# The sixteen tiles of the split activations, laid at sixteen distances of 16 bytes from multiples of 256

## Chip, cores and metric

The kernel runs on one core of one Trainium2 chip. The metric is the device time of one execution in microseconds, the median of several runs. A profile is one such execution, recorded instruction by instruction. On this chip TensorE (PE) multiplies matrices, VectorE (DVE), ScalarE (ACT) and GpSimd (POOL) do element-wise work, and SyncE (SP) starts transfers. SBUF is the on-chip memory: 128 partitions, in each of which an address counts bytes. A tile of 128 rows and 512 fp32 columns takes 2048 bytes of each partition.

## What is computed

A model of two layers on 512 tokens of width 1024. Each layer has a feed-forward block, a mixing block of three token mixers, and a second feed-forward block; a final norm ends it.

```python
for l in range(DEPTH):
    h = rms_norm(x, ffn1_norm[l])
    x = x + 0.5 * swiglu_ffn(h, ffn1_w_gate[l], ffn1_w_up[l], ffn1_w_down[l])
    h = rms_norm(x, mix_norm[l])
    (a_q, a_f, a_i, a_g, b_q, b_k, b_v, b_z, b_beta, b_a,
     c_q, c_k, c_v, c_g) = jnp.split(h @ w_in[l], SPLIT_IDX, axis=-1)
    o_a = hgrn2_mixer(...)
    o_b = gated_deltanet_mixer(...)
    o_c = retention_mixer(...)
    x = x + jnp.concatenate([o_a, o_b, o_c], axis=-1) @ w_out[l]
    h = rms_norm(x, ffn2_norm[l])
    x = x + 0.5 * swiglu_ffn(h, ffn2_w_gate[l], ffn2_w_up[l], ffn2_w_down[l])
return rms_norm(x, final_norm)
```

where `swiglu_ffn(h, wg, wu, wd) = (silu(h @ wg) * (h @ wu)) @ wd`, and the inner width is 2816. All data are fp32.

## The kernel before

The activations lie transposed: eight tiles `x` of 128 features by 512 tokens. For each dense product both factors are split in two parts that TensorE takes in its faster fp32r form: a rounded high part and the remainder as a low part. A product is then three matmuls, high by high, high by low and low by high (`mm3`, line 209), each pair with a weight load of its own. `split_x` (line 386) makes the sixteen tiles of the split activations, `xh0` to `xh7` on ACT and `xl0` to `xl7` on DVE; it is called by `prepare` after each block, once for each of the eight feature tiles. `split` (line 197) does the same for the weights, into tiles `hi` and `lo`.

Three groups of products read the split activations:

- `pg` and `pu`, the gate and up products of the four feed-forward blocks (`ffn`, line 445; matmul at line 215). `hi` or `lo` is stationary, a tile `xh` or `xl` streams through with its 512 columns.
- `ps_fm`, part of the input product of the mixing block (`dense_stream`, matmul at line 258), in the same form.
- `ps_tm`, the other part. Here 128 columns of `xh` or `xl` are stationary, and 256 columns of `hi` or `lo` stream. The first of these, called `t0` in the plan, has 264 columns (8 and 256 side by side).

Other dense products don't read them: `pd`, the down product, streams `ah` and `al`; `ps_out`, the output product, streams `mh` and `ml`. In the mixing block the mixers' own small matmuls, all of them fp32 (line 263), are woven between the matmuls of `ps_fm` and `ps_tm`.

The order on each engine is written by the program's scheduler when it is built. The pools take their memory one behind the other: constants, a pad, the split activations (`xsp`), raw weights, `hi`, `lo`, and the working tiles `m`. With the pad of 224 bytes, `xh0` starts at byte 23296 of a partition, 91 times 256. All sizes behind it are multiples of 256: 2048 for each of the sixteen tiles, 8192 for raw weights, 4352 for a tile `hi` or `lo` (`UNIT` of 1088 columns), 2048 for a working tile. So each of these tiles starts at a multiple of 256. What a matmul reads of them starts there too, since slices are taken at multiples of 512 or 1024 bytes, with one exception. In `t0` the tile `hi` holds four slices of 264 columns, which is 1056 bytes; slice j starts at 1056 j, which is 32 j bytes past a multiple of 256.

```python
t = pool.tile([P, UNIT], F32R, tag=tag, name=tag)
return t[:, 0:shape[1] * shape[2]].rearrange("p (k f) -> p k f", k=shape[1])
...
for j in range(4):
    xh, xl = self.xs[i * 4 + j]
    for m, (a, b) in enumerate(((xh, wh), (xl, wh), (xh, wl))):
        self.mmr(pss[t], a[:, tt], b[:, j, :],
```

Of the kernel before, what the change touches and what calls it, by code (L numbers as in the profile page):

```python
# [11 lines left out]
F32R = mybir.dt.float32r  # L12
# [7 lines left out]
P = 128  # L20
D = 1024
KD = D // P
T = 512
# [73 lines left out]

UNIT = 1088
PAD = 56
STEP = 1600  # L100
SLICE = 2200
LAT = 1.4
# [61 lines left out]
class Kern:  # L164
# [9 lines left out]
    def pool(self, name, bufs, **k):  # L174
        return self.tc.tile_pool(name=name, bufs=bufs, reuse_waits="tile", **k)
# [209 lines left out]

    def split_x(self, d, x, w):
        nc = self.nc
        h = self.xsp.tile([P, T], F32R, tag=f"xh{d}", name=f"xh{d}")
        l = self.xsp.tile([P, T], F32R, tag=f"xl{d}", name=f"xl{d}")
        nc.scalar.activation(h, x, AF.Copy, scale=w[:, d:d + 1])  # L390
        nc.vector.scalar_tensor_tensor(l, x, w[:, d:d + 1], h.bitcast(F32), ALU.mult, ALU.subtract)
        self.xs[d] = (h, l)
# [913 lines left out]
    def interleave(self, dense, waiting):  # L1306
# [3 lines left out]
        while more or any(waiting.values()) or running:  # L1310
# [5 lines left out]
            if r and (r[0] <= self.pe or not more):  # L1316
                self.pe = max(self.pe, r[0])
                self.done = self.pe
                with self.tc.high_priority(offset=PRIO[r[1]]):
                    if next(r[2], self) is self:  # L1320
                        running.remove(r)
                r[0] = max(self.done * LAT + self.pe * (1 - LAT), self.pe) + STEP
                continue
# [97 lines left out]
    def run(self):  # L1421
        nc, tc, io = self.nc, self.tc, self.io
        with ExitStack() as ctx:
# [4 lines left out]
            self.pad = pool("pad", 1)  # L1428
            self.pad.tile([P, PAD], F32, name="pad")
            self.xsp = pool("xsp", 1)  # L1430
# [92 lines left out]
```

## Time and profile before

| | |
|---|---|
| median of 3 runs (lowest, highest) | 2195.98 us (2189.47, 2198.14) |
| the profiled execution, its own time | 2199.5 us |
| its span, first to last instruction | 2197.7 us |
| mean granted TensorE clock | 0.989 |
| PE busy | 2164.1 us (98%), 13079 matmuls |
| DVE, ACT, POOL busy | 1147.4, 842.8, 498.6 us |

The page of the profile gives busy times of the engines, the chain of work that ended last, and groups of instructions. The chain is followed back from the last instruction, at each step to what released it; merged by line, it gives pieces with a start, a length and a count of instructions. The length of a piece over its count is the time from one matmul's start to the next one's. The durations of single matmuls in the groups overlap each other (a matmul of 512 columns has 389 ns there), so pace is read from starts, in the chain or the timeline, and not from durations. The timeline lists single instructions with their start and length in microseconds; PEld is the weight load that goes with a matmul. TensorE's granted clock, as a share of full speed, is 1.00 in nearly all of the span, and 0.50 in short stretches.

### The profile page before, as it was taken

The numbers are of one execution on the slowest core, as the hardware profiler recorded it, in microseconds if no ns is written. First come the engines' busy times: TensorE is split into PE (matmuls) and PEld (weight loads), VectorE is DVE, ScalarE is ACT, GpSimd is POOL, SyncE is SP. The second block draws the span as 40 slices with busy tenths as digits, with TensorE's granted clock in tenths as the row PEclk, the third lists the DMA queues.
The fourth block names the chain that finished last, engine by engine and source line by source line (L and its number), as shares of the span: only waits on it lengthen the run. The fifth ranks groups of instructions, "written<-read, shape, count | busy, mean of one in ns | idle before, by whom it ended". The sixth has DMA issues, their size and how long they took to land.

```text
span 2197.7 us, 31776 instructions
## 1 busy us (share of the span) xinstructions
PE 2164.1 (98%) x13079; PEld 1836.0 (84%) x13079; DVE 1147.4 (52%) x1980; ACT 842.8 (38%) x1319; POOL 498.6 (23%) x466
## 2 busy tenths in 40 slices
PE   8999999998999999999999999999999999999998
PEld 7888888887988788888888888888889888888888
DVE  5544335468497843433543343364866886434335
ACT  4323224555455422222432222254655544223225
POOL 2201012454323210101211010133633412101011
PEclk9999999999999999999999999999999999999999
DMA  5323234221223233232232322242211232323223
GB/s 155 124 79 115 77 106 145 68 78 40 59 59 107 92 100 96 77 115 77 96 115 96 96 96 96 82 150 63 73 45 53 70 106 84 108 94 99 96 86 125
DMA packets 197757, 203.08 MB, mean 92 GB/s; under 512 B 7626, under 2 KB 189292, under 8 KB 197612
## 3 DMA queue, kind: packets, MB, share of 16 engines
q1 hardware_dynamic: 197612, 201.05, 29.0%
q8 instruction: 103, 1.69, 0.3%
q14 instruction: 42, 0.34, 0.1%
HBM read 194.74 MB, written 6.29 MB: 91 GB/s over the span
## 4 chain that ended last, share of the span: by engine, by line
PE 89%; DVE 8%; ACT 1%; issue 1%; POOL 0%; DMA 0%; SPq 0%; DVEq 0%; ACTq 0%; POOLq 0%
PE pd L215 22%; PE pu L215 22%; PE pg L215 21%; PE ps_fm L258 8%; PE ps_tm L258 6%; PE ps_out L258 2%; PE ps_scan L263 1%; DVE aw L147 1%; DVE lo L147 1%; DVE x L147 1%; PE ps_ss L263 1%; PE ps_ao L263 1%; DVE xl L147 1%; PE ps_al L263 0%; PE ps_y L263 0%
## 5 line engine op out<-in xcount | busy, mean ns | idle before, releaser
L147 ACT CAST hi<-raw 128x1024 fp32r<-128x1024 f32 (+2 forms) x369 | 379.1, 1028 | 1104.3 <-PE pg L215 323.1
L147 DVE TENSOR_TENSOR lo<-raw,hi 128x1024 fp32r<-128x1024 f32 (+2 forms) x325 | 391.5, 1205 | 79.4 <-ACT hi L147 66.3
L147 POOL TENSOR_TENSOR g<-g,rstd 128x512 f32<-128x512 f32 x88 | 150.2, 1707 | 1131.9 <-ACT g L144 1131.9
L215 PE MATMUL pd<-ah,hi 128*128 128x512 f32 (+1 forms) x752 | 282.2, 376 | 0.0
L215 PE MATMUL pd<-ah,lo 128*128 128x512 f32 (+1 forms) x752 | 281.8, 375 | 0.0
L215 PE MATMUL pd<-al,hi 128*128 128x512 f32 (+1 forms) x752 | 281.8, 375 | 0.0
L215 PE MATMUL pg<-xl,hi 128*128 128x512 f32 x704 | 275.1, 391 | 1.0 <-DVE xl L147 1.0
L215 PE MATMUL pg<-xh,hi 128*128 128x512 f32 x704 | 274.5, 390 | 0.2 <-ACT xh L147 0.2
L215 PE MATMUL pu<-xh,lo 128*128 128x512 f32 x704 | 274.2, 390 | 0.3 <-DVE lo L147 0.3
L215 PE MATMUL pu<-xh,hi 128*128 128x512 f32 x704 | 274.4, 390 | 0.0
L215 PE MATMUL pg<-xh,lo 128*128 128x512 f32 x704 | 274.2, 390 | 0.0
L215 PE MATMUL pu<-xl,hi 128*128 128x512 f32 x704 | 274.0, 389 | 0.0
L147 DVE TENSOR_TENSOR u<-pu,g 128x512 f32<-128x512 f32 x88 | 60.9, 692 | 280.7 <-PE pu L215 265.2
L147 DVE SCALAR_TENSOR_TENSOR x<-pd,x 128x512 f32<-128x512 f32 (+1 forms) x104 | 67.4, 649 | 230.8 <-PE pd L215 230.5
L147 DVE TENSOR_TENSOR g<-pg,rstd 128x512 f32<-128x512 f32 x88 | 60.8, 691 | 206.8 <-PE pg L215 206.7
L215 PEld LDWEIGHTS pd<-ah,hi 128*128 128x128 f32 x752 | 141.5, 188 | 25.7
L215 PEld LDWEIGHTS pd<-ah,lo 128*128 128x128 f32 x752 | 141.6, 188 | 25.6
L215 PEld LDWEIGHTS pd<-al,hi 128*128 128x128 f32 x752 | 141.5, 188 | 25.5
L215 PEld LDWEIGHTS pg<-xl,hi 128*128 128x128 f32 x704 | 132.2, 188 | 29.4 <-DVE xl L147 2.3
L215 PEld LDWEIGHTS pg<-xh,hi 128*128 128x128 f32 x704 | 132.3, 188 | 27.9 <-ACT xh L147 0.4
L215 PEld LDWEIGHTS pu<-xh,lo 128*128 128x128 f32 x704 | 132.1, 188 | 28.0 <-DVE lo L147 0.8
L215 PEld LDWEIGHTS pu<-xh,hi 128*128 128x128 f32 x704 | 132.1, 188 | 27.7 <-ACT hi L147 0.2
(331 smaller groups left out, 3792.2 us busy)
## 6 DMA issues: line engine op xcount, KB each, us to landing
raw<-in_ffn_w_gate_dram SPq DMA_DIRECT2D x43, 1024.0 KB, 5.2
raw<-in_ffn_w_up_dram SPq DMA_DIRECT2D x43, 1024.0 KB, 5.1
raw<-in_ffn_w_down_dram SPq DMA_DIRECT2D x32, 1024.0 KB, 4.8
raw<-in_w_in_dram SPq DMA_DIRECT2D x20, 1024.0 KB, 5.1
raw<-in_w_in_dram SPq DMA_DIRECT2D x32, 512.0 KB, 3.7
raw<-in_ffn_w_down_dram SPq DMA_DIRECT2D x20, 768.0 KB, 4.4
xd<-x SPq DMA_DIRECT2D x16, 256.0 KB, 2.5
raw<-in_w_out_dram SPq DMA_DIRECT2D x16, 256.0 KB, 2.6
```

What stands on the lines that cost most here:

```text
L147: return f(*args, **kw)
L215: self.nc.tensor.matmul(ps, a[:, k, :], b, start=n == 0, stop=n == 3 * nk - 1)
L258: self.nc.tensor.matmul(ps, a, b, start=start, stop=stop)
L263: self.nc.tensor.matmul(ps, a, b, start=start, stop=stop)
```

## The change

The two tiles of one feature tile become one tile of twice 516 columns: `xh` is its columns 0 to 511, `xl` its columns 516 to 1027, and four columns behind each stay unused. So each of the sixteen tiles starts 2064 bytes behind the one before, which is 8 times 256 and 16 bytes. `xh0` stays at byte 23296; `xh` of feature tile d starts 32 d bytes past a multiple of 256, `xl` 32 d + 16. The sixteen together take 16 times 16, that is 256 bytes more, and every tile behind them moves up by 256 bytes and stays at a multiple of 256. The instructions of each engine and what they wait for stand in the same order as before.

```diff
 UNIT = 1088
 PAD = 56
+
+XSLOT = T + 4
 STEP = 1600
...
     def split_x(self, d, x, w):
         nc = self.nc
-        h = self.xsp.tile([P, T], F32R, tag=f"xh{d}", name=f"xh{d}")
-        l = self.xsp.tile([P, T], F32R, tag=f"xl{d}", name=f"xl{d}")
+        x2 = self.xsp.tile([P, 2 * XSLOT], F32R, tag=f"xs{d}", name=f"xs{d}")
+        h, l = x2[:, 0:T], x2[:, XSLOT:XSLOT + T]
         nc.scalar.activation(h, x, AF.Copy, scale=w[:, d:d + 1])
         nc.vector.scalar_tensor_tensor(l, x, w[:, d:d + 1], h.bitcast(F32), ALU.mult, ALU.subtract)
         self.xs[d] = (h, l)
```

## The prediction

> **What bounds the kernel now.** First the page: span, busy times, and the chain of work that ended last with its shares by engine and by line.
>
> ```profile
> span 2197.7 us, 31776 instructions
> PE 2164.1 (98%) x13079; PEld 1836.0 (84%) x13079; DVE 1147.4 (52%) x1980; ACT 842.8 (38%) x1319; POOL 498.6 (23%) x466
> PE 89%; DVE 8%; ACT 1%; issue 1%; POOL 0%; DMA 0%; SPq 0%; DVEq 0%; ACTq 0%; POOLq 0%
> PE pd L215 22%; PE pu L215 22%; PE pg L215 21%; PE ps_fm L258 8%; PE ps_tm L258 6%; PE ps_out L258 2%; PE ps_scan L263 1%; DVE aw L147 1%; DVE lo L147 1%; DVE x L147 1%; PE ps_ss L263 1%; PE ps_ao L263 1%; DVE xl L147 1%; PE ps_al L263 0%; PE ps_y L263 0%
> ```
>
> TensorE is the path: 89% of the chain. The lines that read the split x are `pu`, `pg`, `ps_fm` and `ps_tm`, together 57% of the span. Next the chain in order of time, which gives the pace of matmuls that wait for nothing (start, length, count).
>
> ```profile
> 65.75 5.44 PE pu L215 x24
> 71.19 5.44 PE pg L215 x24
> 234.89 43.52 PE pd L215 x192
> 2177.53 10.79 PE pd L215 x90
> ```
>
> A matmul of 512 columns follows the one before after 5.44 / 24 = 226.7 ns, the same in `pg`, `pu` and `pd` (43.52 / 192). The last row has 256 columns (the kernel's end): 10.79 / 90 = 119.9 ns. The difference is 106.8 ns for 256 columns, 0.417 ns a column; so 512 columns stream in 213.4 ns, and **13.3 ns a matmul are not streaming**. What are they? The timeline of a stretch at half clock, and the windows row with its clock (the 0.50):
>
> ```profile
> 441.30:443.00 1.70, 1.70 (x6) 1.31 (x5) 1.22 (x7) 0.00 (x0) 0.00 (x0) 0.50 0.41 146
> 441.29 0.63 PE L258 MATMUL ps_fm<-xh,hi 128*128 128x512 f32 x1
> ...
> 443.00 0.63 PE L258 MATMUL ps_fm<-xl,hi 128*128 128x512 f32 x1
> ```
>
> Four matmuls in 1.71 us are 427.5 ns each, and 512 columns at half speed are 426.8 ns. So the 13.3 ns are there at full clock only, where the stream of columns runs fastest. That speaks against a fixed pause and for two readers that get in each other's way: during each matmul the next weights are loaded.
>
> **The change part by part.** No instruction, wait or transfer is added, removed or moved, and all other tiles keep their distance from multiples of 256. What changes is where the 16 tiles start: all at multiples of 256 before, at 0, 16, ... 240 bytes past one now. So there is one term: what the start is worth to one matmul, times the matmuls that read these tiles and stand on the path.
>
> *The value.* One stage of before has its streaming tiles apart already: `t0`, where slice j of `hi` and `lo` starts 32 j bytes past a multiple of 256, and the stationary `xh`, `xl` at multiples of 256. Its timeline (start, length), at the first matmul of each slice, three matmuls each:
>
> ```profile
> 382.87 0.29 PE L258 MATMUL ps_tm<-hi,xh 128*128 128x264 f32 x1
> ...
> 383.24 0.28 PE L258 MATMUL ps_tm<-hi,xh 128*128 128x264 f32 x1
> ...
> 383.60 0.29 PE L258 MATMUL ps_tm<-hi,xh 128*128 128x264 f32 x1
> ...
> 383.97 0.28 PE L258 MATMUL ps_tm<-hi,xh 128*128 128x264 f32 x1
> ...
> 384.32 0.29 PE L258 MATMUL ps_tm<-hi,xh 128*128 128x264 f32 x1
> ...
> 384.69 0.28 PE L258 MATMUL ps_tm<-hi,xh 128*128 128x264 f32 x1
> ...
> 385.05 0.29 PE L258 MATMUL ps_tm<-hi,xh 128*128 128x264 f32 x1
> ...
> 385.42 0.28 PE L258 MATMUL ps_tm<-hi,xh 128*128 128x264 f32 x1
> ...
> 385.78 0.29 PE L258 MATMUL ps_tm<-hi,xh 128*128 128x264 f32 x1
> ...
> 386.15 0.28 PE L258 MATMUL ps_tm<-hi,xh 128*128 128x264 f32 x1
> ...
> 386.51 0.29 PE L258 MATMUL ps_tm<-hi,xh 128*128 128x264 f32 x1
> ...
> 386.87 0.28 PE L258 MATMUL ps_tm<-hi,xh 128*128 128x264 f32 x1
> ...
> 387.23 0.29 PE L258 MATMUL ps_tm<-hi,xh 128*128 128x264 f32 x1
> ```
>
> 36 matmuls take 387.23 - 382.87 = 4.36 us, 121.1 ns each. 264 columns stream in 110.0 ns; 11.1 ns are left. By slice, added over the three rounds and divided by nine: j = 0 (no distance) 1.11 us, 123.3 ns, so 13.3 left, exactly the rest found elsewhere; j = 1 (32 bytes) 1.08 us, 120.0, so 10.0; j = 2 (64) 1.10 us, 122.2, so 12.2; j = 3 (96) 1.07 us, 118.9, so 8.9. Starts are given to 10 ns, so each of these is good to about 1 ns. The aligned slice costs most. I take the mean over the four, a gain of 13.3 - 11.1 = **2.2 ns** a matmul, for all sixteen distances. Distances of 128 and more, and odd multiples of 16, which all `xl` get, no row shows. The bounds: above, all 13.3 ns go; below, as much is lost again, 13.3 ns, where a start costs instead. The value lies where the nearest rows, the four slices, lie.
>
> *How many.* The groups that keep shapes apart, the first and last of `pg` and `pu` (six rows of 704), then those of `ps_fm` and `ps_tm`:
>
> ```profile
> L215 PE MATMUL pg<-xl,hi 128*128 128x512 f32 x704 | 275.1, 391 | 1.0 <-DVE xl L147 1.0
> ...
> L215 PE MATMUL pu<-xl,hi 128*128 128x512 f32 x704 | 274.0, 389 | 0.0
> ...
> L258 PE MATMUL ps_fm<-xh,hi 128*128 128x512 f32 x320 | 133.2, 416 | 1.6 <-issue 1.6
> ...
> L258 PE MATMUL ps_tm<-lo,xh 128*128 128x256 f32 x448 | 130.3, 291 | 0.0
> ```
>
> `pg` and `pu`: 6 x 704 = 4224, nearly all on the path (their 43% of the span are 945 us, and 4224 x 226.7 ns are 958 us). 4224 x 2.2 ns = **9.3 us**. In the mixing block not all count, since in its middle DVE is the path. `ps_fm` has 8% of the span on the chain, 176 us or 776 matmuls at 226.7 ns; `ps_tm` 6%, 132 us or 1099 at 120 ns. Together 1875 of 2496, x 2.2 ns = **4.1 us**. In `ps_tm` it is the stationary side that is moved, and in `t0` both; I take the same value there.
>
> *What is late next.* Nothing, for a gain of 1%: the windows row of four pairs of `pg` and `pu` (length, then busy PE, PEld, DVE, ACT, POOL).
>
> ```profile
> 60.31:103.83 43.52, 43.52 (x193) 35.76 (x192) 18.77 (x23) 13.33 (x18) 9.24 (x6) 1.00 0.39 123
> ```
>
> DVE has 18.77 us of work in 43.52, ACT 13.33, and DMA engines are 39% busy.
>
> *The writers.* ACT and DVE write the 16 tiles, 40 times each in all, now at distances of 16 bytes. For other distances the trace has the convolution's taps, which read `braw` 4 and 8 bytes past a start:
>
> ```profile
> L147 DVE SCALAR_TENSOR_TENSOR bq<-braw,sv_b,bq 128x512 f32<-128x512 f32 x16 | 11.9, 744 | 2.8 <-POOL bq L147 2.7
> L147 DVE SCALAR_TENSOR_TENSOR xl<-ps_x,sv_n,xh 128x512 fp32r<-128x512 f32 x8 | 5.9, 742 | 0.0
> ```
>
> 744 against 742 ns: nothing. Those are reads; if a write paid even 100 ns, 40 of them would be 4 us, and few stand on the path. I take 0.
>
> *The sum.* 9.3 + 4.1 = 13.4 us. The profiled execution has 2199.5 us of its own (span 2197.7 and 1.8 around it) and would have 2186.1. It lies 3.5 us above the median; from the median, 2195.98 - 13.4 = **2182.6 us**, 0.6% faster.
>
> **The rivals.**
>
> *It doesn't matter where the tiles start.* Then the time stays at 2196. For it: `pd`, `pg` and `pu` have one pace to a few tenths of a nanosecond, while the weights they load lie in four buffers 17 x 256 bytes apart. But all of these are multiples of 256, and only `t0` tests anything else. Its slices could differ for their odd length of 264 columns, not for their start; against that stands that slice 0 has just the rest of the others. The Trainium skill speaks for this rival: "SBUF — State Buffer", section "SBUF: two separate sides", says that TensorE never waits for another reader, and names a lock on a port as the one contention among the engines; of the address it says nothing. By that rule the sum would be 0; the slices of `t0` speak against it as far as 264 columns can.
>
> *Odd starts cost.* If the stream is fetched in pieces of 32 bytes or more, a tile that starts in the middle of one has a broken piece at either end. All eight `xl` start so. A third of the 6099 matmuls on the path read `xl`, 2033. At another 13.3 ns each they lose 27.0 us, while the other 4066 gain 2.2 ns, 8.9 us: 18 us slower, 2214. It decides from 4.4 ns per `xl` matmul. Against it: slices 1 and 3 of `t0` start in the middle of 64 bytes and are the fastest two; for it: nothing in the trace starts at 16.
>
> *It gains much more.* If the sixteen distances on the whole do as well as slice 3, the gain is 4.4 ns x 6099 = 27 us, 2169; if all of the rest goes, 81 us, 2115. For it: the rest vanishes at half clock, so it can vanish. Against it: no slice lost more than a third of it. The Trainium skill, "TensorE: Matmul & The Clock Gate", section "Back-to-back issue gap", gives 512 columns at full clock about 215.8 ns. The trace has 226.7; at the page's figure the gain would be an estimated 66 us, 2130.
>
> **How the numbers follow.** Forecast (1 to 4 ns gained) 0.47; no effect 0.25; odd starts cost 0.15; much more 0.13. The forecast's own range is 2172 to 2190. A measurement of this kernel can tell about 0.5%, 11 us, from no change, so 2185 to 2207 is the same. Two thirds of the forecast lie below 2185, 0.31, and with the large gain faster has 0.44; the rest of the forecast, no effect and a small part of the odd starts make 0.43; slower has 0.13. The range of 8 in 10 runs from 2165, which leaves out most of the large gains, to 2206, which leaves out most of the odd starts.
>
> **What would show it.** In the profile after, the pieces of 24 matmuls of `pg` and `pu` should be 5.39 us instead of 5.44 (224.5 ns each), and `pd` should stay at 43.52 for 192. Within a piece the pace should change from tile to tile with the distance. If the pieces stay at 5.44, the start doesn't matter; if matmuls on `xl` alone are slower than 226.7 ns, odd starts cost. If the pace of `pg` falls and the time does not, my share of matmuls on the path is wrong. A changed `pd` would mean that more than the distances changed. The forecast is wrong above all if `t0` is no measure for 512 columns.

## The result, and the profile after

| | before | after |
|---|---|---|
| median of 4 runs (lowest, highest) | 2196.91 us (2189.47, 2198.14) | 2215.53 us (2212.42, 2219.84) |
| ratio after / before, 95% interval | | 1.0093 [1.0064, 1.0122] |
| profiled execution, its span | 2199.5, 2197.7 us | 2216.9, 2215.1 us |
| mean granted clock in it | 0.989 | 0.993 |

The change made the kernel 0.9% slower, where 0.6% faster was forecast. First the page after: span, busy times, chain by engine and by line.

```profile
span 2215.1 us, 31776 instructions
PE 2178.8 (98%) x13079; PEld 1829.5 (83%) x13079; DVE 1146.7 (52%) x1980; ACT 841.8 (38%) x1319; POOL 499.6 (23%) x466
PE 86%; DVE 9%; ACT 2%; issue 1%; DMA 1%; POOL 0%; SPq 0%; DVEq 0%; ACTq 0%; POOLq 0%
PE pu L217 22%; PE pg L217 22%; PE pd L217 21%; PE ps_fm L260 8%; PE ps_tm L260 5%; PE ps_out L260 2%; DVE aw L149 1%; PE ps_scan L265 1%; DVE lo L149 1%; PE ps_ss L265 1%; DVE x L149 1%; PE ps_ao L265 1%; DVE flo L149 1%; DVE ak L149 1%; ACT hi L149 0%
```

DVE, ACT and POOL have the busy times of before to within a microsecond, and TensorE is busy 14.7 us longer with as many matmuls. So the time is in the pace of matmuls. The chain in order of time (start, length, count), after:

```profile
60.74 5.55 PE pg L217 x24
66.30 5.55 PE pu L217 x24
238.05 43.55 PE pd L217 x192
386.84 6.68 PE ps_tm L260 x54
404.22 20.12 PE ps_fm L260 x86
594.96 2.85 PE ps_tm L260 x24
```

and three rows of before that were not shown yet (the `x54` are the longest piece of `t0`):

```profile
381.89 6.59 PE ps_tm L258 x54
399.06 19.73 PE ps_fm L258 x86
591.62 2.87 PE ps_tm L258 x24
```

A piece of 24 matmuls of `pg` or `pu` went from 5.44 to 5.55 us, by the starts in the trace from 226.7 to 231.4 ns a matmul. `ps_fm` lost as much (19.73 to 20.12 us for 86, 4.5 ns each). `pd`, whose streams were not moved, kept its pace. Only the matmuls of `ps_tm` with 256 columns gained: over their unbroken stretches in the traces the mean went from 119.7 to 118.4 ns. `t0`, the stage from which the gain had been read, lost (6.59 to 6.68 us for 54, 1.7 ns each).

These make up the time: 4224 matmuls of `pg` and `pu` at 4.7 ns are 19.9 us, the 776 of `ps_fm` on the path at 4.5 ns 3.5, and the 1099 of `ps_tm` give back 1.4, together 22.0 us. The medians differ by 18.6 and the two spans by 17.4. From their first to their last matmul the feed-forward blocks are 19.4 us longer in the trace after, as the pace says. The mixing blocks are 2.1 us shorter, where the sum would have them 2.1 longer. Nearly all stretches at half clock lie in them, and the clock was lowered for less of the execution after (0.993 against 0.989), so what the pace cost there can't be read from the times.

At half clock nothing was lost. The timeline after, in such a stretch: six matmuls of 512 columns in 2.56 us, 426.7 ns each, as before. The windows row ahead of it shows the clock (the 0.50).

```profile
446.66:449.22 2.56, 2.56 (x7) 1.98 (x6) 1.57 (x10) 0.00 (x0) 0.00 (x0) 0.50 0.47 166
446.66 0.63 PE L260 MATMUL ps_fm<-xs,lo 128*128 128x512 f32 x1
...
449.22 0.63 PE L260 MATMUL ps_fm<-xs,lo 128*128 128x512 f32 x1
```

So three theories stood at the start of the experiments: pace is lost where one stream starts at another distance than the one before it (**unequal starts**); it is set by the distance between a stream's start and the start of the weights, in bytes modulo 256 (**apart from the weights**); or only odd multiples of 16 cost (**odd starts**, the rival whose forecast of 2214 us the result met).

### The profile page after: what moved, and what is told of

It reads as the page before. It is cut to its first block, busy times and chain, and to the rows that moved or that the text cites. A ratio compares the mean times of both kernels' runs of the same rounds, so it can differ in the third digit from the quotient of the medians.

```text
span 2215.1 us, 31776 instructions
## 1 busy us (share of the span) xinstructions
PE 2178.8 (98%) x13079; PEld 1829.5 (83%) x13079; DVE 1146.7 (52%) x1980; ACT 841.8 (38%) x1319; POOL 499.6 (23%) x466
## 4 chain that ended last, share of the span: by engine, by line
PE 86%; DVE 9%; ACT 2%; issue 1%; DMA 1%; POOL 0%; SPq 0%; DVEq 0%; ACTq 0%; POOLq 0%
PE pu L217 22%; PE pg L217 22%; PE pd L217 21%; PE ps_fm L260 8%; PE ps_tm L260 5%; PE ps_out L260 2%; DVE aw L149 1%; PE ps_scan L265 1%; DVE lo L149 1%; PE ps_ss L265 1%; DVE x L149 1%; PE ps_ao L265 1%; DVE flo L149 1%; DVE ak L149 1%; ACT hi L149 0%
## 5 line engine op out<-in xcount | busy, mean ns | idle before, releaser
L217 PE MATMUL pg<-xs,hi 128*128 128x512 f32 x1408 | 443.0, 394 | 1.0 <-DVE xs L149 0.9
L217 PE MATMUL pu<-xs,hi 128*128 128x512 f32 x1408 | 440.5, 393 | 0.4 <-ACT hi L149 0.4
L217 PEld LDWEIGHTS pg<-xs,hi 128*128 128x128 f32 x1408 | 264.9, 188 | 63.0 <-DVE xs L149 1.8
L217 PEld LDWEIGHTS pu<-xs,hi 128*128 128x128 f32 x1408 | 264.0, 188 | 61.7 <-ACT hi L149 0.9
L217 PE MATMUL pu<-xs,lo 128*128 128x512 f32 x704 | 278.0, 395 | 0.0
L217 PE MATMUL pg<-xs,lo 128*128 128x512 f32 x704 | 277.9, 395 | 0.0
L260 PE MATMUL ps_fm<-xs,hi 128*128 128x512 f32 x640 | 208.7, 406 | 1.1 <-issue 1.1
L260 PE MATMUL ps_tm<-hi,xs 128*128 128x256 f32 (+1 forms) x1024 | 195.8, 288 | 0.0
L260 PEld LDWEIGHTS ps_tm<-hi,xs 128*128 128x128 f32 x1024 | 160.5, 190 | 1.3
L217 PEld LDWEIGHTS pg<-xs,lo 128*128 128x128 f32 x704 | 132.3, 188 | 30.7
```

What stands on the lines that cost most here:

```text
L217: self.nc.tensor.matmul(ps, a[:, k, :], b, start=n == 0, stop=n == 3 * nk - 1)
L260: self.nc.tensor.matmul(ps, a, b, start=start, stop=stop)
```

## The experiments

Every kernel here has the instructions of before, in the same order; only addresses differ. In each, all tiles but those named start at multiples of 256. A pace without a quoted row is worked out from the starts of matmuls in the run's trace, the median over the some 40 pieces of a block. Where one time is given, it is that of a single run, beside one of before on the same chip.

**All sixteen tiles at 128, at 32, at 16.** The first two by a longer pad ahead of the tiles and a second one behind them, the third as slices of one large tile.

```diff
-PAD = 56
+PAD = 88
...
             self.xsp = pool("xsp", 1)
+            self.pad2 = pool("pad2", 1)
+            self.pad2.tile([P, 32], F32, name="pad2")
```

(`PAD = 64` and 56 columns behind for 32 bytes.)

```diff
-        h = self.xsp.tile([P, T], F32R, tag=f"xh{d}", name=f"xh{d}")
-        l = self.xsp.tile([P, T], F32R, tag=f"xl{d}", name=f"xl{d}")
+        h, l = (self.xbig[:, o:o + T] for o in XOFF[2 * d:2 * d + 2])
```

> All 16 tiles start 128 bytes past a multiple of 256, everything else stays at multiples of 256. Three theories of the slower pace after the change (a piece of 24 matmuls of pg or pu took 5.44 us before, 5.55 after). 'Unequal starts': pace is lost where one stream starts at another distance than the stream before it; here all are equal, so 5.44 us and a span near 2198. 'Apart from the weights': the distance between a stream's start and that of the weights loaded beside it (0) sets the pace; here it is 128 for all, so the piece is not 5.44; after the change matmuls at 128 took 234, 226, 234 ns, so about 5.5 to 5.6 us and a span of 2205 to 2225. 'Odd starts': only odd multiples of 16 cost, so 5.44 us.

> All 16 tiles start 32 bytes past a multiple of 256, the rest at multiples of 256. Unequal starts: 5.44 us a piece of 24, span near 2198. Apart from the weights: not 5.44; either the 10.0 ns rest of slice 1 of t0 (223.4 ns, 5.36 us, span near 2180) or slower, like the 232 to 236 ns of the tiles at 32 after the change (5.6 us, span near 2225). Odd starts: 5.44.

> All 16 tiles start 16 bytes past a multiple of 256 (slices of one large tile; order and waits of the instructions as before). Unequal starts: 5.44 us a piece, span near 2198. Apart from the weights: not 5.44. Odd starts: every matmul of pg and pu pays, by the price of the prediction 13.3 ns each, 5.76 us a piece and a span near 2275.

The chain of e1, with a piece of `pd` for comparison, then of e2 and of e3:

```profile
160.43 5.60 PE pg L215 x24
238.82 43.53 PE pd L215 x192
```

```profile
66.86 5.60 PE pu L215 x24
```

```profile
159.75 5.56 PE pg L217 x24
```

5.60 us are 233.3 ns (in e1 some pieces have 5.57 to 5.58), 5.56 us are 231.7. With all starts equal, pace is lost all the same: unequal starts are not what it takes. The odd multiple of 16 is the cheapest of the three, and far from the 5.76 us that odd starts would need. The times were 2221.92, 2227.26 and 2214.74 us against 2194.76. Apart from the weights is left. Of the two values that it gave for e2 the slower one came: 32 bytes do not gain, as slice 1 of `t0` had suggested, they cost as much as 128.

**Only `xl` moved, to 128.** The `xl` come from a pool of their own, with a pad of 128 bytes ahead of it and one behind.

```diff
-        l = self.xsp.tile([P, T], F32R, tag=f"xl{d}", name=f"xl{d}")
+        l = self.xsl.tile([P, T], F32R, tag=f"xl{d}", name=f"xl{d}")
```

> The eight xh at multiples of 256, the eight xl 128 bytes past one; the streams then start at 0, 128, 0, 0, 128, 0 and so on. Unequal starts: two of three steps from stream to stream change the distance, so pace is lost about as after the change, 5.5 us a piece or more, on all matmuls around an xl. Apart from the weights: only the matmuls on xl (a third) change, by what e1 shows for one matmul. Odd starts: 5.44 us.

Two pieces of the chain (start, length, count), an early and a later one of the first block, then four matmuls in a row from the timeline (start, length, what it is):

```profile
60.28 5.60 PE pg L215 x24
160.08 5.49 PE pg L215 x24
```

```profile
154.42 0.39 PE L215 MATMUL pu<-xh,hi 128*128 128x512 f32 x1
154.65 0.40 PE L215 MATMUL pu<-xl,hi 128*128 128x512 f32 x1
154.88 0.39 PE L215 MATMUL pu<-xh,lo 128*128 128x512 f32 x1
155.11 0.39 PE L215 MATMUL pu<-xh,hi 128*128 128x512 f32 x1
```

Starts are given to 10 ns; in the pieces of 5.49 us the three intervals are 227 (`xh` by `hi`), 234 (`xl` by `hi`) and 226 ns (`xh` by `lo`). There only the moved tile's matmul pays, and 5.49 us are the mean of 226.7, 233.3 and 226.7 ns to within 0.1 ns. But that holds for two pieces of three. A feed-forward block runs in three groups, each with pieces of `pg` and `pu` and then `pd`. In the first group of each block nearly all pieces are longer at the very same distances: nine of 5.60 us in the first block, with intervals of 236, 234 and 230 ns, and twelve of 5.55 us in each of the others. In these the matmuls on `xh`, at distance 0, pay too, as unequal starts would have it. So the starts of a matmul's own operands do not settle its interval alone; what else counts, no run tells. The time was 2210.52 us.

**Everything moved, by 128.** Here `PAD = 88` stands alone, so raw weights, `hi`, `lo` and the working tiles move with the split x.

> The pad ahead of the tiles is 128 bytes longer: split x, raw weights, hi, lo and all working tiles start 128 bytes past a multiple of 256, so no two of them are apart. If the distance between the stream and the weights sets the pace ('apart from the weights'), pg, pu and pd run at 226.7 ns as before (5.44 us a piece of 24, 43.52 a piece of 192), span near 2198. If the distance of the stream from a multiple of 256 itself sets it ('absolute'), pg and pu have 233.3 ns as in e1 (5.60 us) and pd too (44.8 us), span near 2245.

```profile
59.19 5.44 PE pg L215 x24
954.61 43.52 PE pd L215 x192
2168.12 10.80 PE pd L215 x90
```

All paces are those of before: a shift of 128 bytes common to stream and weights does nothing, where the same shift of the split x alone (e1) cost 6.6 ns. It is the distance between tiles that matters. The time, 2190.27 us against 2196.06, lies within the runs of before.

**The other distances.** The sixteen tiles are slices of one large tile, and the set made for each block gets a shift of its own.

```diff
+SHIFTS = (16, 0, 12, 24, 0, 48)
...
+        if d == 0:
+            self.at = next(self.shifts)
+        h, l = (self.xbig[:, o:o + T] for o in (2 * d * T + self.at, (2 * d + 1) * T + self.at))
```

> All 16 tiles start at one distance, which changes from block to block: 64 bytes in the first feed-forward block, 48 in the second, 96 in the third, 192 in the fourth, 0 in both mixing blocks. A matmul's own distance sets its pace (e4: xl at 128 made 8 ns more, xh at 0 nothing). Expected from the prediction's slices of t0: 64 and 96 slightly below 226.7 ns; expected from e1 to e3: all four between 228 and 235 ns (5.47 to 5.64 us a piece), the span 2205 to 2225.

> As in e6, with 8 bytes in the first feed-forward block, 4 in the second, 160 in the third, 240 in the fourth. If pieces of 16 bytes are what is fetched, 4 and 8 bytes have the pace of 0 (226.7 ns) or a little more for the one broken piece; if the distance counts as such, 4 and 8 lie between 226.7 and the 231.7 ns of 16. 160 and 240 between 228 and 235 ns.

> As in e6, with 80, 112, 176 and 224 bytes in the four feed-forward blocks. Between 228 and 235 ns each (5.47 to 5.64 us a piece), span 2205 to 2225. With e1, e2, e3, e6 and e7 the mean over twelve of the sixteen distances should come to the 231.4 ns that pg and pu have after the change, if each matmul's own distance alone sets its pace.

> As in e6, with 252, 144, 248 and 208 bytes in the four feed-forward blocks: the last two multiples of 16, and starts 4 and 8 bytes ahead of the weights' distance. If 0 is the best of all distances, each is above 226.7 ns; 144 and 208 between 228 and 235. If there is one below 226.7 ns, it is just ahead of 0 (252, 248), since the weight load starts 3 ns behind the stream.

One piece of the chain for the best distance after 0 (e6, 64 bytes) and one for the worst (e7, 4 bytes):

```profile
159.33 5.49 PE pg L217 x24
```

```profile
891.15 5.72 PE pg L217 x24
```

All distances measured, in ns a matmul of 512 columns (0, 16, 32 and 128 from before, e3, e2 and e1), each the median of a block:

| bytes | ns | bytes | ns | bytes | ns | bytes | ns |
|---|---|---|---|---|---|---|---|
| 0 | 226.7 | 64 | 228.9 | 128 | 233.3 | 192 | 233.3 |
| 16 | 231.7 | 80 | 231.1 | 144 | 233.3 | 208 | 234.6 |
| 32 | 233.3 | 96 | 233.3 | 160 | 234.3 | 224 | 233.3 |
| 48 | 233.3 | 112 | 231.1 | 176 | 231.1 | 240 | 233.3 |
| 4 | 238.3 | 8 | 232.3 | 248 | 231.1 | 252 | 231.1 |

At some distances a block has two paces, each steady, and the first group has another than the two behind it. Two pieces of e11 at 208 bytes show it:

```profile
1883.01 5.52 PE pg L217 x24
1970.73 5.63 PE pg L217 x24
```

Twelve pieces have 230.0 ns there and the 28 behind them about 234.7; at 48, 176 and 240 bytes the first twelve have 230.0, 233.3 and 236.7 ns where the table has 233.3, 231.1 and 233.3. Distance 0 is the best of all even so.

The changed kernel has each distance of a multiple of 32 on two matmuls of three and each odd multiple of 16 on one; weighted so, the table gives 232.2 ns, and 231.4 were measured. By the expectation of e8 the two should come out equal if each matmul's own distance alone set its pace, so it does not, and the intervals in the trace after say it more plainly. There the two matmuls on `xh0`, at distance 0, take 230 ns each, not 226.7; `xl0`, at 16 bytes, takes 225, not 231.7; `xl` at 144 bytes takes 226, not 233.3. The table holds for streams that all have one distance; how a mixture comes out is not worked out from it here. Odd multiples of 16 have a mean of 232.5 ns, even ones without 0 232.8: there is nothing in odd starts. Of the expectations, those from `t0` failed (64 and 96 bytes don't gain), and 4 and 8 don't lie between 0 and 16.

**The working tiles moved, by 32.** This is the test of what misled the prediction. A pad of 32 bytes stands ahead of the pool `m` alone. That moves the streams of `pd`, which has 512 columns in most of the kernel and 256 at its end, with the same tiles in the same roles.

```diff
+            self.pad2 = pool("pad2", 1)
+            self.pad2.tile([P, 8], F32, name="pad2")
             self.m = pool("m", M_BUFS)
```

> Only the working tiles are moved, by 32 bytes: the streams ah and al of pd (and mh, ml of ps_out) start 32 bytes past a multiple of 256, split x and all weights at multiples of 256. pg and pu stay at 5.44 us a piece. Any stream of 512 columns apart from its weights: pd goes from 226.7 to 233.3 ns, a piece of 192 from 43.52 to 44.80 us. The kernel's end has pd with 256 columns: if the width decides (256 columns gain, as ps_tm went from 120.0 to 118.4 ns in e2), a piece of 90 goes from 10.79 to 10.66 us; if the role decides (ps_tm gained because there the stationary side was moved), the 256 columns lose like the 512, about 6 ns, 11.3 us. Span near 2207.

```profile
70.54 5.44 PE pg L215 x24
959.07 44.80 PE pd L215 x192
2180.81 10.50 PE pd L215 x90
```

512 columns lose 6.7 ns a matmul (43.52 to 44.80 us), and 256 columns, 32 bytes apart just as they are, gain 3.3 ns (10.79 to 10.50 us). The width of the stream decides the sign, not the role. The time was 2202.67 us against 2198.47, with granted clocks of 0.995 and 0.990, so this pair of times says little about the pace.

**Only the weights' low parts moved, by 128.**

```diff
-        return t[:, 0:shape[1] * shape[2]].rearrange("p (k f) -> p k f", k=shape[1])
+        o = 32 if tag == "lo" else 0
+        return t[:, o:o + shape[1] * shape[2]].rearrange("p (k f) -> p k f", k=shape[1])
```

> Split x and working tiles at multiples of 256; the weights' low parts lo start 128 bytes past one, the high parts hi at one. During the matmul hi by xl the next weights loaded are lo; the matmul lo by xh runs on weights lo and loads hi. If the distance to the weights loaded beside a stream counts, the interval after hi by xl is 234 ns, the other two 227 and 226 (as in e4), 5.49 us a piece of 24. If the distance to the weights in use counts, the interval after lo by xh is the long one. If two of three differ, both count. pd the same, a piece of 192 about 43.9 us; span near 2211.

```profile
60.72 5.55 PE pg L216 x24
967.41 44.37 PE pd L216 x192
```

The intervals are 227 (`xh` by `hi`), 232 (`xl` by `hi`, while `lo` is loaded) and 234 ns (`xh` by `lo`, while `hi` is loaded). Moving the weights costs as moving the stream does, and `pd` pays with the rest (44.37 us for 192). Two of three intervals are long. By the expectation both sets of weights count, those being loaded and those in use; in most pieces of e4, though, where only `xl` was apart, one interval was long. How the two share the loss is open. The time was 2224.73 us against 2198.47.

**Apart where it gains.** All tiles lie as before, but in the products with 256 or 264 columns the stream is set 32 bytes past the weights: `hi` and `lo` start 32 bytes past a multiple of 256 in `ps_tm`, and 224 past one in the kernel's end.

```diff
-                    yield self.split(raw, [P, 4, n])
+                    yield self.split(raw, [P, 4, n], 8)
...
-                return self.end(lambda: self.dense_units(wd[f0 * P:(f0 + nf) * P, :], nf), act, nf)
+                return self.end(lambda: self.dense_units(wd[f0 * P:(f0 + nf) * P, :], nf, at=56), act, nf)
```

> All tiles of before stay; only in the products that stream 256 or 264 columns the stream is set 32 bytes past the weights: hi and lo start 32 bytes past a multiple of 256 in ps_tm (there they stream), and 224 past one in the kernel's end (there they are the weights of pd). If the width of the stream decides, ps_tm goes from 120.0 to about 116.7 ns and the end's piece of 90 from 10.79 to 10.50 us, as pd with 256 columns in e9, while pg, pu, pd and ps_fm keep 5.44 us a piece of 24: 1536 matmuls of ps_tm, 72% of them on the path, and 288 of pd at 3.3 ns make 4.6 us, a span 0.2% shorter and a ratio of 0.998. If in ps_tm only distances as in e2 gain, 1.6 ns, it is 2.8 us, 0.999.

```profile
59.72 5.44 PE pg L215 x24
586.56 2.81 PE ps_tm L258 x24
2170.13 10.50 PE pd L215 x90
```

`ps_tm` with 256 columns went from 119.7 to 117.2 ns in its unbroken stretches, and the end's `pd` gained its 3.3 ns; only the few matmuls of `t0`, with 264 columns, lost a little (6.59 to 6.62 us for 54). So a gain is seen with 256 columns alone. The median is 2190.07 us of 11 runs against 2194.77 of 15, a ratio of 0.9979 [0.9970, 0.9988]. The expectation was 0.998. The gain is small, 4.7 us, and the interval leaves out 1; with the measured paces the sum is 1099 times 2.5 and 288 times 3.3 ns, 3.7 us.

## Why the prediction was wrong, step by step

- **What bounds the kernel** held: TensorE's pace on `pg`, `pu`, `ps_fm` and `ps_tm` is what moved, little else became late (DVE has 9% of the chain after, 8% before), and `pd` kept its pace as long as its own tiles were not moved.
- **That the start matters** held: the pace depends on the distance between stream and weights (e1 to e3, e10), not on addresses as such (e5), and at half clock it doesn't. **That the 13.3 ns are two readers in each other's way** is not shown: with 512 columns no distance took anything off them.
- **The value failed.** The step was "I take the mean over the four, a gain of 13.3 - 11.1 = 2.2 ns a matmul, for all sixteen distances". It was read from streams of 264 columns and put on streams of 512. In place of -2.2 ns the runs show +4.7 in `pg` and `pu` and +4.5 in `ps_fm`. e9 shows the sign turn with the width alone: at 32 bytes, 233.3 against 226.7 ns with 512 columns, 116.7 against 120.0 with 256. The prediction named this as what would make it wrong ("if `t0` is no measure for 512 columns"), and gave it too small a chance. The reading of `t0` itself doesn't stand either. "The aligned slice costs most" took each slice's time for the worth of its distance; in e2 slice 1 is the aligned one, and over the same 36 matmuls it took 118.9 ns and slice 0, at 224 bytes, 122.5. After the change `t0` lost 1.7 ns. One cross-check was missed: it called the bounds 13.3 ns either way, and then let one stage set the sign for all.
- **For `ps_tm` with 256 columns the sign was right:** -1.3 ns where -2.2 was taken. Since `t0`, from which it was read, lost, that was in part luck.
- **The writers** cost nothing, as taken: DVE and ACT are busy no longer than before. The number of writes was off: the trace has 48 of `xh` and 48 of `xl`, not 40 each.
- **The count** of matmuls on the path held for `pg` and `pu`: 4224 at the measured 4.7 ns are 19.9 us, and their blocks are 19.4 us longer. For the mixing blocks it stays open, since the clock differs there.
- **"It doesn't matter"** fell. The Trainium skill's page "SBUF — State Buffer", section "SBUF: two separate sides", by which TensorE waits for no other reader, also lists two read ports for it, one for the stream and one for the weight load, and calls them independent. By that the start would not matter. The traces differ: every distance measured other than 0 cost between 2.2 and 11.6 ns at 512 columns, and the measurement decides.
- **"Odd starts cost"** forecast 2214 us, and 2215.5 was measured; but its mechanism fell. In e3 all tiles are odd and lose 5.0 ns, less than at 32 bytes, and in the trace after the matmuls on `xl` take 229.7 ns in the mean, those on `xh` 232.3. It had put the loss on a third of the matmuls and a gain on the others, and two errors met in the sum. The number was right by luck.
- **"It gains much more"** fell: no distance has less than the 13.3 ns of distance 0 with 512 columns.

## What to carry to other kernels

Before an effect is carried over, ask in what the stage that shows it differs from the stage that is to pay, here 264 against 512 columns, and give the other sign a real chance where one size is all that the trace has. When TensorE is the path, look at its pace from start to start: a few nanoseconds a matmul are a per cent, and where the operands of a matmul start relative to each other can make them without any change in the instructions. In this kernel streams of 512 columns are best at the weights' own distance from a multiple of 256, and streams of 256 columns better 32 bytes past it, the one distance tried for `pd`; for streams of 264 columns no gain was seen.

## What the hardware showed that was not expected

- The pace of matmuls depends on the distance between the starts of streams and weights, from 226.7 ns with all at 0 to 238.3 with all at 4 bytes for 512 columns; moving all tiles together by 128 changes nothing.
- The same distances can have two steady paces in one run (230.0 and 234.7 ns at 208 bytes, 228.9 to 233.3 in e4), and in a mixture of distances a matmul at distance 0 took 230 ns.
- The sign depends on the width: 32 bytes cost 6.7 ns with 512 columns and gain 3.3 ns with 256 (e9).
- Many distances share one pace to a tenth of a nanosecond (233.3 at 32, 48, 96, 128, 144, 192, 224 and 240 bytes; 231.1 at 80, 112, 176, 248 and 252), and single intervals alternate within them (229 and 237 ns in e1).
- Why the distance counts at all, why narrow streams gain, what picks one of two paces, and why two intervals of three are long in e10, no run here tells; that needs one matmul's reads seen by themselves.
